# The second gate of a token mixer's merge: from the Fourier map to the merge

## The chip, the cores and the metric

The kernel runs on one core of a Trainium2 chip. The metric is the device time of one execution in microseconds (us). The engines are named as in the profile: PE is TensorE, DVE is VectorE, ACT is ScalarE, POOL is GpSimd, SP is SyncE. SP, ACT and POOL each have a queue from which DMA transfers are issued in program order.

## The reference

One layer over 2048 latent tokens of width 1024, in float32. What bears on the change is the merge of two token-mixing branches:

```python
p = h @ w_in                                   # one projection for both branches and both gates
attn = attend(q, k, v)                         # latent attention, 8 heads
four = Re(FFT2(p[..., OFF_F:OFF_GA]))          # over positions and over 128 channels of each group
ga = sigmoid(p[..., OFF_GA:OFF_GB])
gb = sigmoid(p[..., OFF_GB:N_IN])
x = x + g1 * ((ga * (attn @ w_o_attn) + gb * (four @ w_fourier)) @ w_out)
# then a second norm, a router and 16 experts of 256 tokens each
```

## The kernel before

The kernel runs in stages, each with its own pools of buffers. The order of the instructions on each engine comes from a scheduler, which follows the written order and moves an instruction up where its buffers allow it.

The input stage (0 to 640 us) projects the tokens with transposed outputs: rows are channels. It writes both gates to the scratch tensors `ga_d` and `gb_d`, 8 blocks of 128 channels by 2048 tokens each. `finish` evacuates a PSUM tile through ACT with a sigmoid, or through DVE without one, and stores it from ACT's queue. For the last five of the eight `gb` blocks the last 512 tokens are projected later, by `gates` in the next stage, and for all eight they are stored without the sigmoid.

Around 640 to 870 us the queries, keys and values are made, and the cosine and sine sums over the positions (`Spectrum`) run beside them.

The Fourier map (L918 to L957) finishes the branch. For each of 8 column blocks `j`, three pieces of 342 frequencies are made: 6 matmuls into `po` (odd part), copied by ACT to `zo`, and 7 matmuls into `pe` (even part). DVE then writes `pe - zo` and `pe + zo` into the halves of `z` (L938, L943). `po` and `pe` have three PSUM buffers each, `z` three, `zo` two. The gate block `gb` (1 MB, two buffers) is loaded by SP (L925), its last quarter gets its sigmoid on ACT (L944), POOL multiplies `z` by it (L945), and ACT's queue stores `z` to `z_d` (L946). In between stand, by program order, the folds of the map's weights for the next blocks (`fold_w`), the split of the first head's keys and values into two parts (`load_kv`, ACT and POOL) and steps of `row_max`, the row maxima of the first query block: score matmuls into `S` (L907) and a maximum on DVE (L908).

The attention (960 to 1832 us) runs 32 groups of 18 key tiles.

The merge (1832 to 2160 us) works in 8 blocks `b` of 256 tokens. For each of four pairs of channel blocks `merge` runs 24 matmuls into `p`, multiplies by `ga` (L1206), adds the gated Fourier branch `zz` (L1207) and splits the sum into `mh` (ACT) and `ml` (DVE). `project` multiplies by `w_out`; the second norm and the router of the previous block lie between. `gates` (L1150) loads `ga` from ACT's queue and `zz` from SP's; both have two buffers, and only the first two pairs are asked for ahead of time (L1158). In the first block the last five rows of `w_out` are loaded, multiplied by a gain on POOL (L1162) and split.

Of the kernel before, what the change touches and what calls it, by code (L numbers as in the profile page):

```python
# [11 lines left out]
F = mybir.dt.float32  # L12
# [5 lines left out]
AF = mybir.ActivationFunctionType  # L18
OP = mybir.AluOpType
# [5 lines left out]
T = 2048  # L25
# [85 lines left out]
def layer_kernel(ctx: ExitStack, tc: tile.TileContext, a: dict, out: bass.AP, stop: str = ""):  # L111
    nc = tc.nc

    def pool(es, name, bufs=1, **kw):
        return es.enter_context(tc.tile_pool(name=name, bufs=bufs, reuse_waits="tile", **kw))
# [14 lines left out]
    gb_d = dr.tile([8, 128, T], F, name="gb_d")  # L130
    z_d = dr.tile([8, 128, T], F, name="z_d")
# [21 lines left out]
    def mm3(ps, terms, extra=()):  # L153

        n = len(terms)
        for i, (lh, ll, rh, rl) in enumerate(terms):
            nc.tensor.matmul(ps, lh, rh, start=i == 0, stop=False)  # L157
            nc.tensor.matmul(ps, lh, rl, start=False, stop=False)  # L158
            nc.tensor.matmul(ps, ll, rh, start=False, stop=i == n - 1 and not extra)  # L159
        for i, (l, r) in enumerate(extra):  # L160
            nc.tensor.matmul(ps, l, r, start=False, stop=i == len(extra) - 1)
# [35 lines left out]
    def load_w(wp, j):  # L197
        raw = wp.tile([128, D], F, name="wraw", bufs=1)
        nc.sync.dma_start(raw, a["w_in_t"][j])
        hi = wp.tile([128, D], R, name="whi")  # L200
        lo = wp.tile([128, D], R, name="wlo")
        split(hi, lo, raw, "a")
        return [x.rearrange("p (k c) -> p k c", k=8) for x in (hi, lo)]

    def terms(w, g):
        return [(w[0][:, k], w[1][:, k], hT[g][0][:, k, :], hT[g][1][:, k, :]) for k in range(8)]

    def finish(ps, g, dst, func=None):

        n = 512 if g < 4 else 256  # L210
        o = st.tile([128, 512], F, name="oA")
        if func is None:
            nc.vector.tensor_copy(o[:, :n], ps[:, :n])
        else:
            nc.scalar.activation(o[:, :n], ps[:, :n], func)
        nc.scalar.dma_start(dst, o[:, :n])

    def tokens(g):
        return slice(g * 512, min((g + 1) * 512, NK))

    def dst_of(j, g):
        if j < 3:
            return cq_d[j, :, tokens(g)]
        return ckv_d[j - 3, :, tokens(g)]

    def gate_dst(j, g):
        return (ga_d if j < 8 else gb_d)[j % 8, :, tokens(g)]

    with ExitStack() as es:
# [7 lines left out]
        def proj(w, g, dst, func=None):  # L237
            n = 512 if g < 4 else 256
            ps = psm.tile([128, 512], F, name="mm")
            mm3(ps[:, :n], terms(w, g))  # L240
            finish(ps, g, dst, func)
# [25 lines left out]
        with ExitStack() as es2, ExitStack() as es_mod, ExitStack() as es_x:  # L267
# [3 lines left out]
            mp = pool(es_mod, "modw", 2, side="right")  # L271
# [115 lines left out]
        with ExitStack() as es2:  # L387
            mp = pool(es2, "mod", 1, side="right")
# [59 lines left out]
            w = load_w(wp, order[0])  # L448
            for n, j in enumerate(order):
                nxt = load_w(wp, order[n + 1]) if n + 1 < len(order) else None  # L450
                if 5 <= j < 9:
                    fourier_fold(j - 5, w)
                elif j < 5:
                    for g in range(4):
                        proj(w, g, dst_of(j, g))
                else:
                    for g in range(4 if j < 20 else 3):
                        proj(w, g, gate_dst(j - 9, g), AF.Sigmoid if j < 17 or g < 3 else None)
                        next(rows, None)
                        next(rows, None)  # L460
                w = nxt
# [72 lines left out]
    with ExitStack() as es:  # L534
# [10 lines left out]
        def gates():  # L545

            for j in range(20, 25):
                w = load_w(wp, j)
                ps = psm.tile([128, 512], F, name="mm")
                mm3(ps, terms(w, 3))  # L550
                finish(ps, 3, gate_dst(j - 9, 3))
                yield

        gate_steps = gates()

        def load_up(name, g, kt, n):
# [187 lines left out]
        ahead = front(0)  # L744
        rows = None
        for t in range(NK // 128):
# [37 lines left out]
            if t % 2 and t + 1 < NK // 128:  # L784
                ahead = front(t + 1)
# [11 lines left out]
    with ExitStack() as es:  # L797
# [50 lines left out]
        def shift_row(i):  # L848

            for c in range(0, NK, 576):  # L850
                nc.vector.memset(kh[i][96:97, c:c + 576].bitcast(F), -1.0)
                yield
                yield
# [65 lines left out]
        with ExitStack() as es2:  # L919
            gp = pool(es2, "gz", 2)  # L920
            psz = pool(es2, "psZ", 1, space=PSUM)
            for j in range(8):
                c = slice(j * 128, (j + 1) * 128)
                gb = gp.tile([128, T], F, name="gb")
                nc.sync.dma_start(gb, gb_d[j])  # L925
                z = gp.tile([128, T], F, name="z", bufs=3)
                zo = gp.tile([128, 1026], F, name="zo")
                for n in range(3):
                    k0 = n * 342
                    k = slice(k0, k0 + 342)  # L930
                    po = psz.tile([128, 512], F, name="po", bufs=3)
                    mm3(po[:, :342], [(WM[0][:, t, c], WM[1][:, t, c], OT[0][:, t, k], OT[1][:, t, k]) for t in range(2)])
                    nc.scalar.copy(zo[:, k], po[:, :342])
                    pe = psz.tile([128, 512], F, name="pe", bufs=3)
                    mm3(pe[:, :342], [(WP[0][:, t, c], WP[1][:, t, c], ET[0][:, t, k], ET[1][:, t, k]) for t in range(2)],
                        [(WN[:, c], NY[:, k])])
                    w = 342 if n < 2 else 341
                    nc.vector.tensor_tensor(z[:, k0:k0 + w], pe[:, :w], zo[:, k0:k0 + w], op=OP.subtract)  # L938
                    u0 = 1 if n == 0 else 0
                    w = 342 if n < 2 else 340  # L940
                    hi = T - (k0 + u0)
                    lo = T - (k0 + w)
                    nc.vector.tensor_tensor(z[:, hi:lo:-1], pe[:, u0:w], zo[:, k0 + u0:k0 + w], op=OP.add)  # L943
                nc.scalar.activation(gb[:, 1536:], gb[:, 1536:], AF.Sigmoid)  # L944
                nc.gpsimd.tensor_tensor(z, z, gb, op=OP.mult)  # L945
                nc.scalar.dma_start(z_d[j], z)  # L946
                if j < 2:
                    fold_w(j + 2)
                if j == 1:
                    for _ in load_kv(0):  # L950
                        pass
                    load_q(0)
                    load_q(1)
                    for _ in shift_row(0):
                        pass
                for _ in range(0 if j < 3 else 2 if j < 5 else 3):
                    next(first, None)  # L957
# [24 lines left out]
    with ExitStack() as es:  # L982
# [117 lines left out]
        for n in range(4 * NH):  # L1100
            nxt = row_max(n + 1) if n + 1 < 4 * NH else iter(())
# [38 lines left out]
    with ExitStack() as es:  # L1140
        wp = pool(es, "wmerge", side="right")
        mp = pool(es, "merge", 2)
# [5 lines left out]
        for k in range(3, 8):  # L1148
            wo.append((wp.tile([128, D], R, name=f"woh{k}"), wp.tile([128, D], R, name=f"wol{k}")))
        def gates(b, j):  # L1150
            ga = mp.tile([128, 2, 256], F, name="ga")
            zz = mp.tile([128, 2, 256], F, name="zz")
            tb = slice(b * 256, (b + 1) * 256)
            nc.scalar.dma_start(ga, ga_d[j:j + 2, :, tb].rearrange("j p t -> p j t"))
            nc.sync.dma_start(zz, z_d[j:j + 2, :, tb].rearrange("j p t -> p j t"))
            return ga, zz

        ahead = [gates(0, 0), gates(0, 2)]  # L1158
# [33 lines left out]
        def merge(b):  # L1192

            tb = slice(b * 256, (b + 1) * 256)
            if b:
                at = at0 if b % 2 == 0 else at1
                nc.sync.dma_start(at, o_d[:, tb].rearrange("(k p) t -> p k t", p=128))
                split(ats[0], ats[1], at, "a")
            ms = (mp.tile([128, 8, 256], R, name="mh", bufs=1), mp.tile([128, 8, 256], R, name="ml", bufs=1))
            for j in range(0, 8, 2):  # L1200
                ga, zz = ahead.pop(0) if ahead else gates(b, j)
                ps = ps1.tile([128, 2, 256], F, name="p1")
                for i in range(2):
                    c = slice((j + i) * 128, (j + i + 1) * 128)
                    mm3(ps[:, i], [(woa[0][:, k, c], woa[1][:, k, c], ats[0][:, k], ats[1][:, k]) for k in range(4)])
                nc.vector.tensor_tensor(ga, ps, ga, op=OP.mult)  # L1206
                nc.vector.tensor_tensor(ga, ga, zz, op=OP.add)  # L1207
                split(ms[0][:, j:j + 2], ms[1][:, j:j + 2], ga, "a")
            return ms
# [106 lines left out]
    with ExitStack() as es:  # L1316
# [147 lines left out]
        for n in range(16):  # L1464
            t = (0, 6, 1, 2, 7, 10, 3, 11, 8, 4, 12, 13, 9, 5, 14, 15)[n]
            for u in range(2):
                nc.tensor.matmul(pi[u], oa[:, t, u].rearrange("p a e -> p (a e)"), ob[:, t, u], start=n == 0, stop=n == 15)
        for u in range(2):
# [3 lines left out]
            with nc.allow_low_precision("whole numbers below 2048"):  # L1472
# [4 lines left out]
                                    op=OP.mult)  # L1477
# [131 lines left out]
```

## Time and profile before

| what | value |
|---|---|
| median of 3 runs | 2821.38 us (2820.79 to 2821.4) |
| the profiled execution: its time | 2819.62 us |
| the profiled execution: its span | 2817.8 us |
| PE busy | 2673.2 us (95% of the span) |
| DVE, ACT, POOL busy | 1810.0, 1398.9, 1018.2 us |
| HBM read and written | 256.59 and 87.08 MB |

The span is the time from the first to the last instruction that the profiler recorded; the execution's own time is 1.8 us longer. A busy share says little about one stage: it is an average over stages with different limits. So the stages are read one by one, and in each the wait that ends last.

### The profile page before, as it was taken

To read this page: it belongs to the slowest core of one execution; us is meant where nothing else is said; L and a number is where in the kernel's file an instruction comes from. 1 tells how busy PE (TensorE), PEld (TensorE's weight loads), DVE (VectorE), ACT (ScalarE), POOL (GpSimd) and SP (SyncE) were. 2 spreads that over 40 slices of the span, in tenths; PEclk is the share of its full clock that TensorE was granted. 3 is DMA by queue.
4 is the path that set the end of the run, shared out by engine and by line. 5 is a ranking of instruction groups with operands and counts; after the bars stand their busy time and mean duration, and the time that the engine had idled before them with its cause. 6 is when DMAs were issued, how large, how long until landed. Compare 5 with 4: busy or idle time off the path is not lost.

```text
span 2817.8 us, 39391 instructions
## 1 busy us (share of the span) xinstructions
PE 2673.2 (95%) x14160; PEld 2209.0 (78%) x14160; DVE 1810.0 (64%) x3272; ACT 1398.9 (50%) x2437; POOL 1018.2 (36%) x840
## 2 busy tenths in 40 slices
PE   6999999999998899999999999999996699999997
PEld 4878777787877677777777777788885599999996
DVE  6632133005667699999999999775556666666663
ACT  6511111114665488888888888722234344444441
POOL 2000000002545688788788787810003311111110
PEclk9999999999999999999999999999998799999999
DMA  6220244124667411011011100164444578787773
GB/s 226 105 78 29 98 159 151 68 82 135 184 180 227 169 31 39 21 38 37 23 49 38 33 23 13 55 214 140 146 136 143 166 227 241 230 234 229 232 224 63
DMA packets 201354, 346.25 MB, mean 123 GB/s; under 512 B 56751, under 2 KB 111731, under 8 KB 199110
## 3 DMA queue, kind: packets, MB, share of 16 engines
q1 hardware_dynamic: 151958, 235.52, 26.9%
q0 software_dynamic: 14832, 46.55, 7.3%
q10 hardware_dynamic: 34368, 61.66, 6.1%
q8 instruction: 111, 1.82, 0.3%
q14 instruction: 85, 0.70, 0.1%
HBM read 256.59 MB, written 87.08 MB: 122 GB/s over the span
## 4 chain that ended last, share of the span: by engine, by line
PE 79%; DMA 7%; DVE 7%; issue 3%; POOL 2%; ACT 2%; SPq 0%; POOLq 0%; ACTq 0%; DVEq 0%
PE mm L157 6%; PE mm L158 6%; PE mm L159 6%; PE S L907 5%; PE P L1083 4%; PE P L1084 4%; PE P L1082 4%; PE Ob L1023 4%; PE Oa L1022 4%; PE pa L158 4%; PE pa L159 4%; PE pa L157 4%; PE p L157 3%; PE p L159 3%; PE p L158 3%
## 5 line engine op out<-in xcount | busy, mean ns | idle before, releaser
L147 POOL TENSOR_TENSOR acc<-acc,phi 128x512 f32<-128x512 f32 x384 | 495.6, 1291 | 77.1 <-ACT phi L143 57.8
L144 DVE TENSOR_TENSOR plo<-P,phi 128x512 fp32r<-128x512 f32 x576 | 385.5, 679 | 20.9 <-ACT phi L143 18.9
L908 DVE TENSOR_REDUCE mxs<-S 128x1 f32<-128x1024 f32 (+1 forms) x384 | 365.7, 952 | 45.8 <-PE S L907 39.2
L1085 ACT ACTIVATE P<-P 128x512 f32<-128x512 f32 x576 | 328.9, 586 | 72.1 <-PE P L1084 68.4
L143 ACT CAST ewhi<-ewraw 128x1024 fp32r<-128x1024 f32 x181 | 190.1, 1050 | 312.8 <-PE pa L158 191.6
L143 ACT CAST phi<-P 128x512 fp32r<-128x512 f32 x576 | 327.7, 593 | 16.1 <-ACT P L1085 0.7
L157 PE MATMUL mm<-hh,whi 128*128 128x512 f32 (+1 forms) x792 | 312.5, 396 | 0.0
L158 PE MATMUL mm<-hl,whi 128*128 128x512 f32 (+1 forms) x792 | 311.3, 394 | 0.0
L159 PE MATMUL mm<-hh,wlo 128*128 128x512 f32 (+1 forms) x792 | 310.0, 392 | 0.0
L144 DVE TENSOR_TENSOR ewlo<-ewraw,ewhi 128x1024 fp32r<-128x1024 f32 x181 | 219.0, 1222 | 131.5 <-ACT ewhi L143 131.4
L158 PE MATMUL pa<-xTl,ewhi 128*128 128x256 f32 x1024 | 290.5, 284 | 3.8 <-DVE xTl L144 3.6
L157 PE MATMUL pa<-xTh,ewhi 128*128 128x256 f32 x1024 | 291.2, 285 | 0.0
L159 PE MATMUL pa<-xTh,ewlo 128*128 128x256 f32 x1024 | 289.4, 283 | 0.0
L1082 PE MATMUL P<-qh,kh 97*128 97x512 f32 x576 | 230.2, 400 | 1.3 <-DVE qh L914 1.3
L1083 PE MATMUL P<-ql,kh 96*128 96x512 f32 x576 | 228.7, 397 | 0.0
L1084 PE MATMUL P<-qh,kl 96*128 96x512 f32 x576 | 228.2, 396 | 0.0
L907 PE MATMUL S<-kh,qh 96*128 96x512 f32 (+1 forms) x640 | 200.0, 377 | 17.5 <-DVE mxs L908 13.9
L1023 PE MATMUL Ob<-plo,vv 128*66 128x512 f32 x576 | 215.8, 400 | 0.2 <-DVE plo L144 0.2
L1022 PE MATMUL Oa<-phi,vv 128*128 128x512 f32 x576 | 214.9, 399 | 1.0 <-ACT phi L143 1.0
L615 POOL TENSOR_TENSOR ckv<-ckv 128x256 f32<-128x256 f32 x9 | 6.9, 762 | 567.7 <-ACT ckv L613 567.7
L158 PEld LDWEIGHTS pa<-xTl,ewhi 128*128 128x128 f32 x1024 | 193.8, 189 | 9.9 <-DVE xTl L144 7.7
L157 PEld LDWEIGHTS pa<-xTh,ewhi 128*128 128x128 f32 x1024 | 193.3, 189 | 2.2 <-ACT xTh L143 0.2
(499 smaller groups left out, 5864.0 us busy)
## 6 DMA issues: line engine op xcount, KB each, us to landing
ewraw<-in_w_gate_t_dram SPq DMA_DIRECT2D x64, 512.0 KB
ewraw<-in_w_up_t_dram SPq DMA_DIRECT2D x64, 512.0 KB
ewraw<-in_w_e_down_dram SPq DMA_DIRECT2D x64, 512.0 KB
wmr<-in_w_mod_dram SPq DMA_DIRECT2D x64, 256.0 KB
wraw<-in_w_in_t_dram SPq DMA_DIRECT2D x30, 512.0 KB
wm<-in_w_mod_t_dram SPq DMA_DIRECT2D x32, 256.0 KB
ga_d<-oA ACTq DMA_DIRECT2D x32, 256.0 KB
gb_d<-oA ACTq DMA_DIRECT2D x32, 256.0 KB
```

What stands on the lines that cost most here:

```text
L143: (nc.scalar.copy if eng == "a" else nc.vector.tensor_copy)(hi, src)
L144: nc.vector.tensor_tensor(lo, src, hi.bitcast(F), op=OP.subtract)
L147: nc.gpsimd.tensor_tensor(o, x, y, op=op)
L157: nc.tensor.matmul(ps, lh, rh, start=i == 0, stop=False)
L158: nc.tensor.matmul(ps, lh, rl, start=False, stop=False)
L159: nc.tensor.matmul(ps, ll, rh, start=False, stop=i == n - 1 and not extra)
L907: nc.tensor.matmul(S[:, d:e], q[:96, j * 128:(j + 1) * 128], k[:96, c0 + d:c0 + e], start=True, stop=True)
L908: nc.vector.tensor_reduce(mxs[:, c:c + 1], S[:, :w], axis=AX.X, op=OP.max)
L1082: nc.tensor.matmul(S, k[:, c], qh, start=True, stop=False)
L1083: nc.tensor.matmul(S, k[:96, c], ql, start=False, stop=False)
L1084: nc.tensor.matmul(S, l[:, c], qh[:96], start=False, stop=True)
L1085: nc.scalar.activation(S, S, AF.Exp)
```

## The change

In the input stage every gate tile that is projected there now gets its sigmoid on the way out. Only the last 512 tokens of the last five `gb` blocks are still stored without it. The map loads just these (`gl`, five tiles of 256 KB), takes the sigmoid, and stores them back to `gb_d` from POOL's queue. The map's result goes to `z_d` ungated, also from POOL's queue; the load of 1 MB per block and the product on POOL are gone there. The merge loads `gb` beside `ga` and `zz`, with three buffers each, and POOL multiplies `zz` by it. Each pair is asked for two pairs ahead, across block borders.

```diff
@@ input stage
-                        proj(w, g, gate_dst(j - 9, g), AF.Sigmoid if j < 17 or g < 3 else None)
+                        proj(w, g, gate_dst(j - 9, g), AF.Sigmoid)
@@ Fourier map
+            gl = [gp.tile([128, 512], F, name=f"gl{j}", bufs=1) for j in range(3, 8)]
+            for j in range(3, 8):
+                nc.sync.dma_start(gl[j - 3], gb_d[j, :, 1536:])
             for j in range(8):
                 c = slice(j * 128, (j + 1) * 128)
-                gb = gp.tile([128, T], F, name="gb")
-                nc.sync.dma_start(gb, gb_d[j])
...
-                nc.scalar.activation(gb[:, 1536:], gb[:, 1536:], AF.Sigmoid)
-                nc.gpsimd.tensor_tensor(z, z, gb, op=OP.mult)
-                nc.scalar.dma_start(z_d[j], z)
+                nc.gpsimd.dma_start(z_d[j], z)
+                if j > 2:
+
+                    nc.scalar.activation(gl[j - 3], gl[j - 3], AF.Sigmoid)
+                    nc.gpsimd.dma_start(gb_d[j, :, 1536:], gl[j - 3])
@@ merge
         def gates(b, j):
-            ga = mp.tile([128, 2, 256], F, name="ga")
-            zz = mp.tile([128, 2, 256], F, name="zz")
+            ga = mp.tile([128, 2, 256], F, name="ga", bufs=3)
+            gb = mp.tile([128, 2, 256], F, name="gb", bufs=3)
+            zz = mp.tile([128, 2, 256], F, name="zz", bufs=3)
             tb = slice(b * 256, (b + 1) * 256)
+            nc.sync.dma_start(gb, gb_d[j:j + 2, :, tb].rearrange("j p t -> p j t"))
             nc.scalar.dma_start(ga, ga_d[j:j + 2, :, tb].rearrange("j p t -> p j t"))
             nc.sync.dma_start(zz, z_d[j:j + 2, :, tb].rearrange("j p t -> p j t"))
+            nc.gpsimd.tensor_tensor(zz, zz, gb, op=OP.mult)
             return ga, zz
...
-                ga, zz = ahead.pop(0) if ahead else gates(b, j)
+                ga, zz = ahead.pop(0)
+                nxt = b * 4 + j // 2 + 2
+                if nxt < T // 64:
+                    ahead.append(gates(nxt // 4, nxt % 4 * 2))
```

The scheduler moves instructions with it. On ACT, from the third column block of the map on, before (`qh` and `vv` are splits of the first queries and values):

```order
L933 COPY zo<-po 128x342 x3
L944 ACTIVATE gb<-gb 128x512 x2
L150 CAST vv_7148<-vraw 128x6x64
L933 COPY zo<-po 128x342
L150 CAST qh<-qraw 96x512
L933 COPY zo<-po 128x342
L946 DMA z_d<-z 128x2048
L933 COPY zo<-po 128x342 x2
```

and now, at the same place and up to the attention's table load:

```order
L150 CAST kh_7146<-kraw 96x384 x2
L948 ACT_TABLE_LOAD
L948 ACTIVATE gl_7200<-gl_7200 128x512
L143 CAST wph<-wt 128x2x256
L934 COPY zo<-po 128x342 x2
L143 CAST wmh<-xc 128x2x256
L150 CAST vv_7148<-vraw 128x6x64
L948 ACTIVATE gl_7201<-gl_7201 128x512
L948 ACTIVATE gl_7202<-gl_7202 128x512
L934 COPY zo<-po 128x342
L948 ACTIVATE gl_7203<-gl_7203 128x512
L948 ACTIVATE gl_7204<-gl_7204 128x512
```

The sigmoids now stand together in the middle of the map, behind two key copies; the stores of `z` have left ACT's queue, and after one more copy of queries fifteen `zo` copies follow each other.

On POOL, from the start of the map, before (`kl`, `vv`, `ql` are the low parts of keys, values and queries):

```order
L812 MEMSET vv_7148 128x18x2
L945 TENSOR_TENSOR z<-z,gb 128x2048
L147 TENSOR_TENSOR kl_7147<-kraw,kh_7146 96x384 x2
L945 TENSOR_TENSOR z<-z,gb 128x2048
L147 TENSOR_TENSOR kl_7147<-kraw,kh_7146 96x384 x4
L147 TENSOR_TENSOR vv_7148<-vraw,vv_7148 128x6x64 x2
L147 TENSOR_TENSOR ql<-qraw,qh 96x512 x2
```

and now:

```order
L147 TENSOR_TENSOR kl_7147<-kraw,kh_7146 96x384 x4
L945 DMA z_d<-z 128x2048
L147 TENSOR_TENSOR kl_7147<-kraw,kh_7146 96x384
L147 TENSOR_TENSOR vv_7148<-vraw,vv_7148 128x6x64
L147 TENSOR_TENSOR kl_7147<-kraw,kh_7146 96x384
L147 TENSOR_TENSOR vv_7148<-vraw,vv_7148 128x6x64
L147 TENSOR_TENSOR ql<-qraw,qh 96x512
L945 DMA z_d<-z 128x2048
```

The products are gone, and the stores of `z` stand between the splits; the five gate stores (L949) follow a little later, ahead of the third store of `z`.

On SP, at the start of the merge (`x` is first a buffer for rows of `w_out`), before:

```order
L1180 DMA rc<-in_norm_g_dram 128x8x1
L1155 DMA zz<-z_d 128x2x256 x2
L1161 DMA x<-in_w_out_dram 128x1024 x3
L1155 DMA zz<-z_d 128x2x256 x2
L1175 DMA h_18019<-in_norm_g_dram 128x1024
```

and now:

```order
L1186 DMA rc<-in_norm_g_dram 128x8x1
L1158 DMA gb<-gb_d 128x2x256
L1160 DMA zz<-z_d 128x2x256
L1158 DMA gb<-gb_d 128x2x256
L1160 DMA zz<-z_d 128x2x256
L1167 DMA x<-in_w_out_dram 128x1024 x3
L1158 DMA gb<-gb_d 128x2x256
```

Two gate loads have come ahead of the weights. POOL's products stand likewise: two of `zz` before the first three of `x`, one between these and the last two, and one behind them.

## Rows read from the trace of the kernel before

**Rows 1.** Stages; columns: stretch, length, busy of PE PEld DVE ACT POOL, PEclk, DMA

```profile
865.00:960.00 95.00, 74.46 (x388) 67.32 (x387) 64.12 (x106) 36.10 (x73) 54.78 (x28) 0.89 0.72 245
...
1832.00:2160.00 328.00, 312.61 (x1813) 269.33 (x1811) 199.78 (x395) 94.83 (x150) 25.27 (x25) 0.97 0.46 149
```

**Rows 2.** The same view, slices of 5 us inside the map

```profile
885.00:890.00 5.00, 3.14 (x18) 2.85 (x17) 4.94 (x7) 0.45 (x1) 3.94 (x3) 0.93 0.57 172
...
915.00:920.00 5.00, 1.82 (x12) 1.54 (x11) 0.44 (x2) 0.00 (x0) 4.28 (x1) 1.00 0.95 398
```

**Rows 3.** Waits around the map: who <- for whom, total us, times, longest

```profile
ACT gb L944 <- DMA gb<-gb_d: 23.0, 5, 6.2
...
DVE z L938 <- ACT zo L933: 18.0, 6, 5.8
...
PE S L907 <- DVE mxs L908: 11.3, 5, 5.7
...
ACT L1085 <- POOL z L945: 8.3, 1, 8.3
```

**Rows 4.** Timeline of PE: start, length, engine, line, operation, [idle before <- releaser]

```profile
873.17 0.42 PE L157 MATMUL po<-oth,wmh 128*128 128x342 f32 x1 [1.70 <-ACT wmh L143]
...
943.09 0.62 PE L907 MATMUL S<-kh,qh 96*128 96x512 f32 x2
...
943.55 0.32 PE L157 MATMUL pe<-eth,wph 128*128 128x342 f32 x1
...
946.70 0.63 PE L907 MATMUL S<-kh,qh 96*128 96x512 f32 x2
...
953.80 0.76 PE L1082 MATMUL P<-qh,kh 97*128 97x512 f32 x1 [1.06 <-DVE qh L914]
```

**Rows 5.** Timeline of ACT at the end of the map

```profile
955.75 0.33 ACTq L946 DMA_DIRECT2D z_d<-z  x1
...
956.16 1.28 ACT L1085 ACT_TABLE_LOAD   x1 [8.26 <-POOL z L945]
...
957.46 1.07 ACT L1085 ACTIVATE P<-P 128x512 f32<-128x512 f32 x2
```

**Rows 6.** Timelines of POOL and DVE, fold and gate early in the map

```profile
876.45 0.69 DVE L144 TENSOR_TENSOR wml<-xc,wmh 128x512 fp32r<-128x512 f32 x1
...
881.34 4.78 POOL L945 TENSOR_TENSOR z<-z,gb 128x2048 f32<-128x2048 f32 x1 [0.17 <-ACT wph L143]
...
881.55 5.11 DVE L144 TENSOR_TENSOR wpl<-wt,wph 128x512 fp32r<-128x512 f32 x1
```

**Rows 7.** Timeline of POOL: first sum of the attention after the map

```profile
959.77 1.26 POOL L147 TENSOR_TENSOR acc<-phi 128x512 f32<-128x512 f32 x1 [1.45 <-DMA z_d<-z]
```

**Rows 8.** Loads issued by POOL: issue ns min/median/max; then size and us to landing

```profile
L491 POOL DMA_DIRECT2D tabx<-in_c_so_dram x4: 729/736/743, 825.4 to 854.6; - x4
...
tabx<-in_c_so_dram POOLq DMA_DIRECT2D x4, 512.0 KB, 6.2
```

**Rows 9.** Page, groups: POOL additions of 128x512

```profile
L147 POOL TENSOR_TENSOR acc<-acc,phi 128x512 f32<-128x512 f32 x384 | 495.6, 1291 | 77.1 <-ACT phi L143 57.8
```

**Rows 10.** Merge, first block: slice of 8 us, then timelines of POOL and DVE

```profile
1852.00:1860.00 8.00, 5.15 (x14) 3.80 (x15) 7.96 (x6) 2.60 (x4) 5.42 (x2) 0.71 0.91 269
...
1840.20 7.96 POOL L1162 TENSOR_TENSOR x<-x,g 128x1024 f32<-128x1024 f32 x3 [6.88 <-DMA x<-in_w_out_dram]
...
1843.04 2.87 DVE L1207 TENSOR_TENSOR ga<-ga,zz 128x512 f32<-128x512 f32 x1
```

**Rows 11.** Merge, later blocks: slice, then timelines of DVE and PE

```profile
1932.00:1940.00 8.00, 6.14 (x23) 4.54 (x23) 4.45 (x13) 2.13 (x3) 0.00 (x0) 0.83 0.54 180
...
1933.56 0.69 DVE L1206 TENSOR_TENSOR ga<-p,ga 128x512 f32<-128x512 f32 x1 [2.29 <-DMA ga<-ga_d]
...
2012.91 0.68 DVE L144 TENSOR_TENSOR ml<-ga,mh 128x512 fp32r<-128x512 f32 x1
...
2015.01 0.39 PE L159 MATMUL p<-woh,ml 128*128 128x512 f32 x1
```

## The prediction

> **What bounds the kernel now.** I read the stages first. TensorE (PE) is busy 74.46 of the 95 us around the Fourier map at a mean granted clock of 0.89, and 312.61 of the 328 us of the merge [rows 1]; nowhere else does the change move anything but the order of a few rows. So there are 20.5 us of idle PE, and some lost clock, to be had in the map, and 15.4 us in the merge. Inside the map the slices show PE at 3.14 of 5 us from 885 and 1.82 of 5 us from 915 [rows 2]. The waits name the cause: ScalarE (ACT) waits 23.0 us, five times, for the gate tile `gb` to land, in order to take the sigmoid of its last quarter; VectorE (DVE) then waits 18.0 us for the copy `zo`, which stands behind that sigmoid in ACT's queue; PE waits 11.3 us for DVE's row maxima, which stand behind the `z` additions [rows 3]. It is one chain: load, sigmoid, copy, addition, PSUM buffer free, matmul. The load itself waits for one of two `gb` buffers, which the GpSimd (POOL) product gives back. A second wait comes early: a fold subtraction of DVE with both inputs in SBUF takes 0.69 us alone, but 5.11 us when it starts 0.2 us after a POOL product of 4.78 us [rows 6]. At the stage's end ACT waits 8.3 us for the last product, because the store of `z` stands in its queue; so the first exponentials start at 957.46, although the first scores were started at 953.80 [rows 3 to 5].
>
> **The map, term by term.** From the first map matmul at 873.17 to the first score matmul at 953.80 are 80.6 us [rows 4]. What PE has to do in it: 24 pieces of 13 matmuls, 312; from 943.55 to 946.70 stand 20 of them without a wait, 0.1575 us each [rows 4], so 49.1 us. The row maxima of the first query block take 8 pairs of 512 columns at 0.46 us (943.09 to 943.55 [rows 4]) and 4 singles at half of that, 4.6 us; with four transposes some 0.5 us more. Work: 54.2 us. The other 26.4 us are waits and low clock.
>
> Removed are the eight loads of 1 MB, the eight products and the eight stores in ACT's queue; with them goes every wait of the chain above, and the blocked folds. What is late next: (a) the tail after the last map matmul, now 946.70 to 953.80 [rows 4], 7.1 us, of which one pair, one single and the transposes, 1.2 us by the figures above, are work; part of the other 5.9 is the backlog on DVE, so I keep 4 us of waiting. (b) ACT copies the keys in program order ahead of the `zo` of the third column block, so it waits for a key load that starts only when POOL has split the first chunk; three `po` buffers cover most of it; I take 2 us. (c) `z` has three buffers, and a buffer is free when its store has landed. The stores now stand in POOL's queue, behind splits of keys and five small gate stores. An issue there takes 0.74 us, and a 512 KB load of that queue lands in 6.2 us on a busy memory system [rows 8]; the same 1 MB store from ACT was issued at 955.75 and had landed by 959.77, 4.0 us [rows 5, 7]. By these two rows the new store takes 4 to 12 us (twice the half-size load); I take 6, since the map leaves the memory system freer. A buffer comes round after three blocks of 39 matmuls, 18.4 us, and a few maxima, some 20 us; I take 0.5 us of wait. Sum: 54.2 + 4 + 2 + 0.5 = 60.7, a gain of 19.9 us; rounded for smaller misses to **19**. Bounds: 54.2 + 4 = 58.2 gives 22.4; with every store at 12 us and the key wait at 6 us it is some 69, a gain of 12.
>
> The exponentials can then follow the first scores without the 1.28 us table load and the store in front of them [rows 5]. That is up to 2 us, but four score buffers hide part of it, and the first low parts of the probabilities may lie where the last `z` waits for its store, which costs up to 2 us. I take 0.5 us of gain, bounds -2 to +2. In the input stage three evacuations move from DVE to ACT beside PE's matmuls: nothing, as both engines idle there; uncovered they would be 3 x 0.6 us. The attention is PE's own, with other neighbours in its queues: 0, give or take 1.
>
> **The merge.** Added are 32 loads of 256 KB, 32 POOL products of 128x512 elements at 1.29 us each (41 us; a POOL operation of that size is the nearest row [rows 9]) and third buffers. In the first block the product stands in front of everything: POOL does two of them before the weight products `x`, one between, one after, and the `x` loads stand behind two more gate loads in SyncE's queue. There POOL and DVE already take turns: three weight products run from 1840.20 to 1848.2, an addition that is normally 0.69 takes 2.87 us, and PE idles 2.85 us of the slice at 1852 [rows 10]. The price lies between 0 (the loads land while POOL waits for `x`, 6.88 us [rows 10]) and all four products plus 1 us of loads, 6.2 us; I take 3.
>
> In the seven later blocks the third buffers and the early loads remove waits like the 2.29 us for `ga` at 1933.56, which left PE idle 1.86 us [rows 11]: a gain of about 2 in all. Against it stands the port. The rows show that a DVE operation with both inputs in SBUF waits out a POOL product [rows 6, 10]. The Trainium skill says the same as a rule (SBUF — State Buffer, "Who interferes with whom"): a DVE instruction with two SBUF inputs and a GpSimd instruction that reads SBUF exclude each other for the whole instruction, whoever starts first. By that rule each of the 32 new products can hold up an addition, an `ml` subtraction or a norm.
> In one undisturbed block the last `ml` ended at 2013.6 and was first used by PE at 2015.0: slack 1.4 us [rows 11]. One collision of 1.29 us per block is covered; the earlier `ga` adds to the slack. A second one would cost 7 x 1.2 = 8 us. I take 0.5. Merge in sum: +3 - 2 + 0.5 = **+1.5**, bounds -4 to +14.
>
> **Sum.** -19 - 0.5 + 1.5 = -18 us. The profiled execution took 2819.62, so 2801.6; the median of the runs is 1.76 above it, so 2803.4, said as **2803.5**.
>
> **Rivals.**
> (1) *The stores keep the map late.* POOL works its queue in order, so `z` of the first blocks leaves only after the key splits, and five small stores go before the third. If each store takes 12 us, DVE finds no `z` buffer in blocks 3 to 5 and the map gains 12 instead of 19; the merge's terms stay. -12 + 1.5 = -10.5, about 2811. For it: 13 issues in POOL's queue where none were; against it: the 20 us from buffer to buffer.
> (2) *The port gives the gain back, and more.* Each merge product runs while DVE wants the port, four times in every block: 7 x (4 x 1.29 - 1.4) = 26 us, and 6 us in the first block, without the 2 us of gain: +32. With the map's -19.5 that is +12.5, about 2834, slower than before. It decides once the merge loses more than 25 us, which is over 3.2 collisions per block if the start costs 6. With 2.5 to 3 per block (7 x (3.2 - 1.4) = 13 to 7 x (3.9 - 1.4) = 17, and the start 5) the sum is -2 to +3, no change. For it: the addition of 2.87 us in rows 10; against it: two of the four products of a block fall, by the loads that release them, into the projection, where DVE has little to do. By the Trainium skill's rule as it stands this rival is what should happen to those products that meet a DVE operation; the time is the one worked out here.
> (3) *The loads also relieve the merge.* The products hide, the first block is no later, and the clock stays up in the map: -22 - 1 - 3, about 2796.
> (4) *The early loads do nothing* that the buffers did not give already: then the 2 us of the later blocks are missing, 2805.5; this lies inside the forecast.
>
> **How the numbers follow.** Forecast with (4), 2798 to 2808.5: 0.62. Rival (1), 2808.5 to 2815.5: 0.17. Rival (3), below 2798: 0.08. Rival (2): about no change 0.07, slower 0.06. A measurement of this kernel can tell about 0.2%, 5.6 us, from no change: faster means below 2815.7. So faster 0.62 + 0.17 + 0.08 = 0.87, same 0.07, slower 0.06. The range leaves out rival (2) and the lower half of (3): 2796 to 2815.
>
> **What would show it.** In the changed profile the map should have no ACT wait for a gate before a `zo`, PE idle of under 10 us and its first score matmul near 934; the exponentials should follow it within 2 us. If `z` additions wait for a DMA, rival (1) is at work. In the merge, many additions or `ml` subtractions of near 2 us, and PE waiting for `ml`, would show rival (2). A merge that is longer than 328 us by over 5, or shorter by over 4, would make the merge term wrong. The whole is wrong if the stretch from the first map matmul to the first score does not shrink by at least 12 us.

## The result and the profile after

The changed kernel takes 2835.57 us (median of 7 runs, 2830.39 to 2846.08), the kernel before, run beside it, 2821.38 (7 runs, 2813.62 to 2827.96): a ratio of 1.0051, interval 1.003 to 1.0072. It is slower by half a per cent, where 18 us less were forecast.

The stages are cut at the same instructions in both traces: the first map matmul, the first and the last score matmul `P`, the transposition of `aff` that ends the merge, the first `pa` matmul of the experts.

| stretch | before, us | after, us | difference | forecast |
|---|---|---|---|---|
| up to the first map matmul | 873.2 | 876.8 | +3.6 | 0 |
| map | 80.6 | 64.9 | -15.7 | -19 |
| attention | 867.7 | 898.8 | +31.1 | -0.5 |
| last score matmul to the end of the merge | 336.4 | 345.0 | +8.6 | +1.5 |
| routing | 62.6 | 62.4 | -0.2 | 0 |
| experts | 597.3 | 596.4 | -0.9 | 0 |

The sum is +26.5 us and not +14.2, because the profiled execution of after (2846.08 us) was the slowest of its seven, while that of before was 1.8 us under its median. The first line is no effect of the change: in the eight traces below it lies between 868.9 and 876.7 us in the six that have the changed input stage, and at 869.1 and 872.7 in the two that have the old one.

So the map gained somewhat less than was forecast, and a stage that the diff does not touch lost twice as much. The view of stretches for the map, the attention and the merge (length, busy time of PE, PEld, DVE, ACT, POOL with counts, granted clock, DMA share, GB/s), first before, then after:

```profile
873.20:953.80 80.60, 62.27 (x336) 57.78 (x337) 55.00 (x86) 26.84 (x54) 49.08 (x22) 0.90 0.69 235
953.80:1821.50 867.70, 862.21 (x3790) 660.15 (x3791) 794.54 (x1224) 712.66 (x1350) 697.39 (x560) 1.00 0.13 34
1821.50:2157.90 336.40, 321.99 (x1864) 276.44 (x1862) 202.98 (x401) 99.25 (x159) 29.97 (x25) 0.97 0.46 148
```

```profile
876.80:941.70 64.90, 57.02 (x336) 54.64 (x336) 51.92 (x86) 25.41 (x51) 21.97 (x27) 0.95 0.64 216
941.70:1840.50 898.80, 879.18 (x3790) 662.97 (x3791) 787.44 (x1224) 719.91 (x1350) 696.43 (x559) 0.98 0.12 32
1840.50:2185.50 345.00, 321.88 (x1864) 273.99 (x1862) 214.33 (x401) 99.02 (x159) 75.13 (x57) 0.98 0.52 169
```

In the attention PE has the same 3790 records. Its idle time rose from 5.5 to 19.6 us, and its busy time by 17.0 us at a granted clock of 0.98 instead of 1.00: half of the loss is waiting, the other half the same matmuls at a lower clock after the waits.

What waits there is told by the list of waits of the attention (who, for whom, total us, times, longest), of which these rows bear on it, before:

```profile
POOL t L1075 <- DMA rb<-r_d: 20.2, 16, 3.0
ACT ah L143 <- POOL acc L147: 8.8, 8, 3.3
PE S L907 <- DVE mxs L908: 4.0, 13, 0.8
```

and after:

```profile
ACT ah L143 <- POOL acc L147: 46.8, 24, 4.9
DVE al L144 <- ACT ah L143: 25.3, 12, 4.2
POOL t L1078 <- DVE plo L144: 23.7, 7, 4.3
POOL t L1078 <- DMA rb<-r_d: 19.6, 8, 4.1
PE S L907 <- DVE mxs L908: 18.7, 13, 3.5
```

`t` is a group's output, `rb` the reciprocal of its sums, loaded by SP in 64 copies. `acc` is the running sum of a group's probabilities, `ah` and `al` are its high and low parts. The product of `t` and `rb` on POOL (L1075, now L1078) belongs to the group before. The order of POOL's queue tells what moved. Before, for one group (`ql` is a split of the next queries):

```
L147 TENSOR_TENSOR acc<-acc,phi 128x512 x12
L147 TENSOR_TENSOR ql<-qraw,qh 96x512
L1075 TENSOR_TENSOR t_10149<-t_10149,rb 64x512
L147 TENSOR_TENSOR acc<-phi 128x512
```

and after:

```
L147 TENSOR_TENSOR acc<-acc,phi 128x512 x9
L1078 TENSOR_TENSOR t_10137<-t_10137,rb 64x512
L147 TENSOR_TENSOR acc<-acc,phi 128x512 x3
L147 TENSOR_TENSOR ql<-qraw,qh 96x512
```

The product has gone ahead of the last three additions of the group in 20 of 31 cases, and ahead of the last one once. No line of the attention was edited; the scheduler moved it. Why it did is not shown. One such place on the chip, from the timelines of SP, POOL, ACT, DVE and PE after (start, length, engine, line, operation, [idle before <- releaser]):

```profile
1074.27 0.46 SPq L1070 DMA_DIRECT2D rb<-r_d  x1
...
1077.99 1.27 POOL L1078 TENSOR_TENSOR t<-t,rb 64x512 f32<-64x512 f32 x1 [4.16 <-ACT qh L150]
1079.23 3.99 POOL L147 TENSOR_TENSOR acc<-acc,phi 128x512 f32<-128x512 f32 x3
...
1083.25 0.62 ACT L143 CAST ah<-acc 128x512 fp32r<-128x512 f32 x1 [4.83 <-POOL acc L147]
...
1083.90 0.82 DVE L144 TENSOR_TENSOR al<-acc,ah 128x512 fp32r<-128x512 f32 x1 [4.13 <-ACT ah L143]
...
1085.91 1.22 PE L907 MATMUL S<-kh,qh 96*128 96x512 f32 x2 [3.43 <-DVE mxs L908]
1086.93 0.63 PE L1086 MATMUL P<-ql,kh 96*128 96x512 f32 x1
```

POOL stands still for 4.16 us until `rb` lands, 3.7 us after its issue (the row names a copy that ended just then; that it is the load is settled by e7). Behind it stand three additions, behind them `ah` in ACT's queue with the next exponentials, behind that `al` and the row maxima on DVE, and then PE. PE's next matmuls take 0.63 us, where the same one took 0.40 before the stall. Taking all rows together, whatever releaser they name, POOL stands idle in front of `t` for 40.4 us before and 66.4 us after. In front of a group's first addition such a wait is harmless: in e1 below it still adds up to 34.0 us there, and the attention loses nothing.

In the map, the rows that answer to [rows 2, 4, 5]: waits of the stretch, then DVE, PE and ACT.

```profile
PE pe L157 <- DVE z L944: 4.3, 1, 4.3
```

```profile
895.16 3.73 DVE L144 TENSOR_TENSOR wml<-xc,wmh 128x512 fp32r<-128x512 f32 x1
...
901.20 0.66 PE L157 MATMUL pe<-eth,wph 128*128 128x342 f32 x1 [4.31 <-DVE z L944]
...
941.74 0.77 PE L1085 MATMUL P<-qh,kh 97*128 97x512 f32 x1 [1.06 <-DVE qh L914]
...
943.43 1.28 ACT L1088 ACT_TABLE_LOAD   x1 [8.15 <-PE P L1087]
944.73 0.58 ACT L1088 ACTIVATE P<-P 128x512 f32<-128x512 f32 x1
```

No wait for a gate is left in it, and of 18.3 us of idle PE (80.60 - 62.27) 7.9 remain (64.90 - 57.02). In the merge, the groups of DVE and POOL (busy us, mean ns), first before, then after:

```profile
L1207 DVE TENSOR_TENSOR ga<-ga,zz 128x512 f32<-128x512 f32 x32 | 25.7, 805 | 0.6
...
L1243 DVE TENSOR_TENSOR h<-h,wraw 128x1024 f32<-128x1024 f32 x14 | 17.1, 1220 | 0.2
```

```profile
L1216 DVE TENSOR_TENSOR ga<-ga,zz 128x512 f32<-128x512 f32 x32 | 29.4, 920 | 2.2 <-POOL zz L1161 1.2
...
L1252 DVE TENSOR_TENSOR h<-h,wraw 128x1024 f32<-128x1024 f32 x14 | 22.8, 1626 | 0.2
...
L1161 POOL TENSOR_TENSOR zz<-zz,gb 128x512 f32<-128x512 f32 x32 | 47.6, 1496 | 224.9 <-DVE h L1251 115.7 <-DMA zz<-z_d 80.5 <-DVE ga L1215 11.2
```

With the same 401 instructions DVE is busy 214.33 us instead of 202.98: two groups with both inputs in SBUF have grown by 3.7 and 5.7 us, and POOL's products take longer than their size would (1496 ns; 1291 ns is POOL's mean for an addition of that size [rows 9]).

### The profile page after: what moved, and what is told of

The parts are those of the page before. It is cut to its first block, busy times and chain, and to the rows that moved or that the text cites. A ratio compares the mean times of both kernels' runs of the same rounds, so it can differ in the third digit from the quotient of the medians.

```text
span 2844.3 us, 39571 instructions
## 1 busy us (share of the span) xinstructions
PE 2686.0 (94%) x14160; PEld 2208.0 (78%) x14160; DVE 1813.3 (64%) x3269; ACT 1405.9 (49%) x2437; POOL 1035.4 (36%) x877
## 3 DMA queue, kind: packets, MB, share of 16 engines
q1 hardware_dynamic: 160230, 236.84, 26.8%
## 4 chain that ended last, share of the span: by engine, by line
PE 50%; DVE 7%; POOL 4%; issue 3%; DMA 3%; ACT 2%; SPq 0%; POOLq 0%; DVEq 0%; ACTq 0%
PE S L907 4%; PE pa L158 4%; PE pa L159 4%; PE pa L157 4%; PE P L1085 4%; PE P L1086 4%; PE P L1087 4%; PE Oa L1025 4%; PE Ob L1026 4%; POOL acc L147 2%; PE p L159 2%; PE p L158 2%; PE p L157 2%; PE py L1555 2%; PE py L1557 2%
## 5 line engine op out<-in xcount | busy, mean ns | idle before, releaser
L158 PEld LDWEIGHTS pa<-xTl,ewhi 128*128 128x128 f32 x1024 | 194.2, 190 | 11.4 <-DVE xTl L144 9.0
```

## The experiments

Two theories stood at the start. **O**: the place of `t`'s product in POOL's queue costs the attention its 31 us. **W**: the other rows that the scheduler moved there cost them. For the merge: **P**, the products hold DVE up, against **L**, the added loads do. In the table the stretches are cut as above; a ratio is to the kernel before, run on the same chip beside it (a median of 2816.76 to 2818.15 us beside e1 to e8). Each stretch comes from one trace. e4 leaves out the merge's second gate, e7 the division by the sums; the others compute the whole result.

| kernel | us | ratio, 95% interval | map | attention | merge |
|---|---|---|---|---|---|
| before | 2821.38 | | 80.6 | 867.7 | 336.4 |
| after | 2835.57 | 1.0051 (1.003, 1.0072) | 64.9 | 898.8 | 345.0 |
| e1: `t` late | 2808.03 | 0.9966 (0.9951, 0.998) | 65.5 | 864.6 | 346.2 |
| e2: `t` later | 2806.91 | 0.9964 (0.9951, 0.9977) | 66.3 | 867.8 | 345.8 |
| e3: store alone | 2852.22 | 1.0135 (1.0114, 1.0155) | 85.4 | 897.1 | 337.5 |
| e7: `t` early, no wait | 2807.16 | 0.995 (0.9932, 0.9967) | 66.2 | 866.4 | 345.7 |
| e4: no product | 2792.33 | 0.9926 (0.9905, 0.9947) | 66.3 | 865.0 | 332.3 |
| e5: product on DVE | 2791.88 | 0.9905 (0.9888, 0.9921) | 66.3 | 865.0 | 332.1 |
| e8: ahead alone | 2814.59 | 0.9988 (0.9974, 1.0001) | 81.2 | 865.4 | 330.9 |
| e6: gate in the map | 2810.1 | 0.9967 (0.9956, 0.9978) | 79.8 | 865.2 | 329.8 |

**e1.** The product is put where it stood before, by an order that the scheduler must keep:

```diff
-                yield
-                yield
-                yield
-                yield
-                nc.gpsimd.tensor_tensor(t[0], t[0], rb, op=OP.mult)
+                tc.keep_in_program_order(nc.gpsimd.tensor_tensor(t[0], t[0], rb, op=OP.mult))
```

> The changed kernel with one thing held: the attention's rescaling product of POOL (t by rb, L1078) is kept three additions later in POOL's queue, in front of the first addition of a group, where it stands in the kernel before. All else of the change stays, and hardly a row moves on ACT and DVE. Theory O (the order): the product, put in front of the last three additions of most groups, waits there for the load of rb; the additions, the copy ah, the exponentials and the row maxima wait behind it. Then the attention returns from 899 us to 867 to 870 us, PE's waits for the row maxima there from 18.7 to under 6 us, and the time is the median of the changed kernel less 18 to 30 us: 2806 to 2818, faster than before or about the same. Rival W (wider): the other instructions that the scheduler moved on ACT and DVE in the attention cost the 31 us; then the attention stays at 890 us or more, and the time above 2828.

Measured: 2808.03 us, and 864.6 us for the attention. PE's wait for the row maxima in that stretch, 18.7 us in after, is now:

```profile
PE S L907 <- DVE mxs L908: 1.4, 3, 0.9
```

The attention is even a little shorter than the 867 to 870 us expected. W falls. It was a serious rival: by the traces, some 157 of DVE's 1224 operations in the attention, 193 of ACT's 1350 and 22 of POOL's stand in another place of their queue after than before. From after to e1 only 3, 6 and 22 move, and the whole loss is gone. By the ratios (1.0051 - 0.9966) the place of this one instruction costs about 24 us in a typical execution.

**e2.** As e1, with all seven `yield` kept, so that the product follows four key tiles later.

> The same with the product four key tiles later still, behind the fourth addition of the group, where rb should have landed long before. Theory O: POOL's wait for rb (some 20 us in 16 waits in the kernel before, harmless there) goes away, and the attention takes the same 867 to 870 us as with the product in front of the group, within 2 us, since that wait held up nothing that PE needs; time within 3 us of the run with the product in front of the group. Rival: the wait in front of the group also cost PE something; then the attention is 3 us or more shorter and so is the time.

POOL no longer stands idle in front of `t` at all; the time is that of e1 within 1.1 us, and the attention is 3.2 us longer, not shorter, at 867.8 about the same as before. So the wait in front of the group cost nothing that can be seen.

**e3.** One part alone, in the kernel before:

```diff
-                nc.scalar.dma_start(z_d[j], z)
+                nc.gpsimd.dma_start(z_d[j], z)
```

> The kernel before with one part of the change alone: the map's result, still gated, is stored from POOL's queue in place of ACT's. With it the scheduler moves the rescaling product three additions forward in the same groups as in the changed kernel. Theory O: the attention becomes 885 to 900 us, the map gets 0 to 8 us shorter (the store no longer holds ACT up, the load of the gate still does), the merge stays at 336 us: time 2828 to 2845, slower than before. Rival N: the loss in the attention came from the rest of the change (ungated map, gate loads, lookahead); then the attention stays at 868 us and the time at 2812 to 2822.

The attention takes 897.1 us, as O says: another edit, the same order of all operations there as in the changed kernel, the same loss. As the map is longer here and not shorter, a map that is shorter on the chip is not what moves `t`. The map, however, got 4.8 us longer, and so the time is above the range. There the rows of DVE and POOL show why:

```profile
892.66 2.90 POOL L147 TENSOR_TENSOR kl<-kraw,kh 96x384 fp32r<-96x384 f32 x3
895.53 1.81 POOL L147 TENSOR_TENSOR vv<-vraw,vv 128x384 fp32r<-128x384 f32 x2
897.31 2.47 POOL L147 TENSOR_TENSOR ql<-qraw,qh 96x512 fp32r<-96x512 f32 x2
...
893.37 6.96 DVE L144 TENSOR_TENSOR wml<-xc,wmh 128x512 fp32r<-128x512 f32 x1
...
902.64 0.66 PE L157 MATMUL pe<-eth,wph 128*128 128x342 f32 x1 [11.73 <-DVE z L943]
```

A subtraction that takes 0.69 us alone [rows 6] ends only when POOL's seven splits are through, and PE then has idled 11.7 us.

**e7.** The changed kernel with the product early in every group (the nine `yield` between the store of `r_d` and the product are gone; in the trace it is ahead of three additions in 30 of 31 groups), and nothing to wait for:

```diff
-                nc.gpsimd.tensor_tensor(t[0], t[0], rb, op=OP.mult)
+                tc.keep_in_program_order(nc.gpsimd.tensor_tensor(t[0], t[0], t[0], op=OP.mult))
```

> The changed kernel with the attention's rescaling product early in all groups (three additions ahead of a group's end, where the changed kernel has it in 21 of 31), but multiplying t by itself, so that it has nothing to wait for from the load of rb (the division by the sums is left out; the load of rb is still made). Theory W (wait): the loss comes from the wait for rb alone; the attention takes 863 to 870 us and the time is that of the run with the product held late, 2803 to 2813. Rival S (slot): the product's own 1.3 us ahead of the last additions is too much for POOL, or the rest of the order is; then the attention stays at 880 us or more and the time above 2822.

Attention 866.4 us, time 2807.16, both in the range of theory W, which here is the wait: it is the wait for `rb`, not the slot. (With one input the product is a little shorter, 1.03 us.)

**e4.** e1 without the line of the merge's product; the gate is still loaded.

> The run with the rescaling product held in front of the group, and the 32 gate products of the merge left out (the output then lacks the second gate); the gate is still loaded. Theory P (port): the products cost the merge what they hold up on DVE, about 1.2 us in each later block and some of the 4.7 us of the first; without them the merge is 334 to 338 us in place of 345, and the time 7 to 11 us under that of the run with the products. Rival L (loads): the merge is longer by the added gate loads ahead of the weights and by the order alone; then it stays at 342 to 346 us and the time within 3 us of that run.

The merge falls by 13.9 us to 332.3, more than either theory had: P in direction, and under-priced. L has little left: with all the added loads the stage is 4 us shorter than before, and only 1.4 us longer than that of e8, which asks ahead as early and loads no gate.

**e5.** e1 with the product on DVE:

```diff
-            nc.gpsimd.tensor_tensor(zz, zz, gb, op=OP.mult)
...
+                ga, gb, zz = ahead.pop(0)
+                nc.vector.tensor_tensor(zz, zz, gb, op=OP.mult)
```

> As the run with the rescaling product held (2808.0, merge from the last score matmul to the router's end 346 us), with the merge's 32 gate products on DVE, each just ahead of its pair's matmuls, in place of POOL. Without any product this stage took 332 us and the kernel 2792.3, so the products on POOL cost 14 us. Theory P (port): on POOL they cost that by holding up DVE operations with both inputs in SBUF; on DVE they cost their own 0.7 us each, 22 us in all, most of it beside PE's matmuls: merge 333 to 340 us, time 2794 to 2802. Rival Z (late data): whoever makes the product, the sum waits for it and for its loads, and DVE's queue is the bound; then the merge is 344 us or more and the time 2806 or more.

The merge takes 332.1 us, as without any product and a little under the range. The group of DVE:

```profile
L1203 DVE TENSOR_TENSOR zz<-zz,gb 128x512 f32<-128x512 f32 x32 | 23.9, 746 | 10.8 <-DMA zz<-z_d 10.8
```

23.9 us of work on the busier engine are hidden, where 47.6 us on the idle one cost 14. What the products cost on POOL is, in large part, what they hold up on DVE: with the same 401 operations DVE is busy 216.79 us in the merge of e1 and 200.86 in that of e4. Up to the first `mh` matmul of the second block e1 takes 74.3 us and e4 67.9, from there to the end of the merge 271.9 and 264.4. In the later blocks the hold-up can be followed to PE. `x1Tl` is an input of the router's matmuls; PE's wait for it, in e1 and then in e5:

```profile
PE p L1268 <- DVE x1Tl L144: 5.2, 5, 1.2
```

```profile
PE p L1268 <- DVE x1Tl L144: 0.5, 1, 0.5
```

One of the five places in e1, from the timelines of POOL, DVE and PE:

```profile
2000.44 3.67 POOL L1157 TENSOR_TENSOR zz<-zz,gb 128x512 f32<-128x512 f32 x2 [5.36 <-DVE ga L1211]
...
2001.19 1.78 DVE L1212 TENSOR_TENSOR ga<-ga,zz 128x512 f32<-128x512 f32 x1
2002.89 1.27 DVE L144 TENSOR_TENSOR x1Tl<-p,x1Th 128x512 fp32r<-128x512 f32 x2
...
2003.62 1.24 PE L1268 MATMUL p<-x1Tl,wr 128*16 128x256 f32 x8 [1.20 <-DVE x1Tl L144]
```

An addition of 0.69 us takes 1.78 beside two products, `x1Tl` follows it in DVE's queue, and PE idles 1.20 us. In the first block the products also stand between POOL's weight products, and no run separates that order from the hold-up of DVE. This version is the fastest that computes the whole result: 0.9905 of the time before.

**e8.** The kernel before, with only the merge's three buffers and loads two pairs ahead.

> The kernel before with one part of the change alone: ga and zz of the merge with three buffers and asked for two pairs ahead; the gate stays in the map. The prediction's term was a gain of 2 us in the later blocks. Theory A: the stage from the last score matmul to the router's end goes from 336 to 331 to 334 us, as in the runs without a product on POOL, and the time falls by 2 to 5 us. Rival: the two waits that it removes are given back elsewhere; then the stage stays within 1 us of 336 and the time within 1 us of before.

The stage is 5.5 us shorter, the kernel 3.0 us (interval 0.9974 to 1.0001, so just not told from no change). For the stage other traces agree: 329.8 us in e6, which has the same merge, and 337.5 in e3, which has that of before. The term of 2 us was too small.

**e6.** e1 with the gate back in the map, but out of ACT's way: the last quarters in tiles of their own, products and store in POOL's queue, none in the merge. `w` is 2048 in the first three blocks and 1536 in the others.

```diff
+                gb = gp.tile([128, T], F, name="gb")
+                nc.sync.dma_start(gb[:, :w], gb_d[j, :, :w])
...
+                if j > 2:
+                    nc.scalar.activation(gl[j - 3], gl[j - 3], AF.Sigmoid)
+                    nc.gpsimd.tensor_tensor(z[:, w:], z[:, w:], gl[j - 3], op=OP.mult)
+                nc.gpsimd.tensor_tensor(z[:, :w], z[:, :w], gb[:, :w], op=OP.mult)
                 nc.gpsimd.dma_start(z_d[j], z)
```

> A version meant to keep both gains: the map is gated on POOL as in the kernel before, but nothing of the gate stands in ACT's way any more (the last quarters are small tiles of their own with their sigmoid early, products and store both in POOL's queue); the merge loads only ga and zz, with three buffers and two pairs ahead, and has no product; the attention's rescaling product is held in front of the group. If the map's loss in the kernel before came from ACT waiting for the gate's load, the map takes 65 to 72 us, the merge 331 to 335, the time 2790 to 2800. Rival: the 1 MB loads of the gate, or POOL's eight products of 4.8 us beside DVE's folds, cost the map by themselves; then it takes 75 us or more and the time is 2802 or more.

A miss: the map takes 79.8 us, although ACT waits for a gate only once, 3.4 us, where it waited five times and 23.0 us before [rows 3]. Three of the map's waits:

```profile
PE pe L157 <- DVE z L952: 10.3, 2, 5.2
...
ACT vv L150 <- DMA vraw<-v_d: 8.6, 1, 8.6
...
ACT gl L955 <- DMA gl<-gb_d: 3.4, 1, 3.4
```

Timelines of POOL and DVE:

```profile
897.74 1.98 POOL L147 TENSOR_TENSOR kl<-kraw,kh 96x384 fp32r<-96x384 f32 x2
899.68 4.54 POOL L957 TENSOR_TENSOR z<-z,gb 128x2048 f32<-128x2048 f32 x1
904.18 0.92 POOL L147 TENSOR_TENSOR vv<-vraw,vv 128x384 fp32r<-128x384 f32 x1
905.06 0.58 POOL L958 DMA_DIRECT2D z_d<-z  x1
...
897.98 8.14 DVE L836 TENSOR_TENSOR xc<-xc 128x512 f32<-128x512 f32 x1
```

So ACT's wait for the gate, which the prediction took for the main cause in the map, is not all of it: with most of that wait gone the map keeps nearly its old length. Over half of PE's 18.6 us of idle time, 10.3 us, stand behind folds that DVE ends late beside POOL's work. That the products alone do it is not shown: the loads of the gate are back as well, and ACT waits 8.6 us for a load of values, with `zo` copies behind it for which PE then waits 2.8 us. What the change gains in the map comes from taking away loads, products and ACT's wait together.

## Why the prediction was wrong

- **Map** (60.7 us, bounds to 69; gain 19, 12 to 22.4): within the bounds, 64.9 to 66.3 in six traces, a gain of 14 to 16. PE is busy 57.0 us and not 54.2, at a granted clock of 0.95. Of its 7.9 us of idle time 3.6 are the tail, for which 4 were taken; the key wait (2) and the wait for a `z` buffer (0.5) do not show at PE. The rest is a stall of 4.3 us behind the fold subtraction of 3.73 us, which the sum does not have: the prediction had said that the blocked folds go with the products, but POOL's splits of values and queries stand beside this one. The tells held: no wait of ACT for a gate, idle PE under 10 us; the first score matmul came at 941.7 instead of 934, 3.6 us of it from the later start.
- **Stores** (rival 1): rejected. They land in 5.6 us (6 were taken), and no `z` addition waits for a DMA.
- **Start of the exponentials** (gain 0.5, bounds -2 to +2): the size was right, the reason not. They start 3.0 us behind the first score matmul instead of 3.7; the table load of 1.28 us is still there (943.43), only the store in front of it is gone, and so the tell of 2 us did not hold.
- **Attention** ("0, give or take 1"): this step failed, by 31 us in the trace and some 24 us typically (e1). The reason given was that it is PE's own. What it left out is that the scheduler had reordered POOL's queue there, and that a queue in order, in which an instruction waits for a load, holds three other engines. The prediction weighed the order rows of the map and of the merge; of all other stages it said that "the order of a few rows" moves, and gave that no price. In the attention one product that moved up by three additions was the price.
- **Merge** (+1.5, bounds -4 to +14): 8.6 us, and 9.8 in e1; within the bounds, but over the 5 us by which the prediction itself would call the term wrong, and two errors offset each other in it. The loads ahead and the buffers give 5.5 us (e8), not 2. The products cost 13.9 us (e1 less e4), and the gate loads 1.4 (e4 less e8), where both together were put at 3.5; 6.4 of the 13.9 fall up to the second block and 7.5 behind it, where 0.5 was taken. The slack of 1.4 us for one collision per block was read at `ml`, but the products fall on the norm as well, where the operation with `wraw` went from 1.22 to 1.63 us, 14 times, which is half of DVE's extra 11.4 us, and on additions with the router's `x1Tl` behind them (e5).
- **Rival 2** (the port): the mechanism was right, and e4 and e5 show it. Its size, 32 us, was more than twice too large (13.9, e1 less e4), and it alone would not have made the kernel slower: with `t` in place 9.6 us of gain are left with the products on POOL (e1), and 26.8 with them on DVE (e5).
- **Slower at all**: "slower" had been given to rival 2 alone. The kernel is slower through an instruction that no term or rival named. Rival 3 (the products hide) and rival 4 (the early loads do nothing) fall with the numbers of the merge.

These two gains are the ratios of e1 and e5, 0.34% and 0.95% of 2821.4 us; the forecast was 18.

## What to carry to other kernels

Where a scheduler sets the order, an edit in one stage can move instructions in another: read the whole difference of order, and look first for an instruction that waits for a load and has gone up in a busy in-order queue; hold it in place. The engine with the most idle time need not be the cheapest home for an elementwise product: here products with both inputs in SBUF, put on GpSimd, cost VectorE's time as well, and on VectorE itself they were free.

## What the runs showed of the hardware

- **DVE can be held through several POOL operations in a row.** In e6 one operation took 8.14 us beside four POOL operations, in e3 6.96 us beside seven; each ended 0.5 to 1.1 us after the last of them. It is not always so: in the kernel before, the subtraction of 5.11 us [rows 6] ended 0.6 us after the one product, although POOL's next operation had begun at 886.07, with no gap. Nor does a pause of POOL always let DVE in: the subtraction of 3.73 us after, from 895.16, spans an issue of 0.59 us at 895.55 and ends behind the two splits that follow. What decides is not shown. The Trainium skill (SBUF — State Buffer, "Who interferes with whom") says that the shared pair is held for the whole instruction and that the order of issue decides; the traces agree that one holds up the other, but the measured waits in e3 and e6 are longer than any one POOL instruction there, and the measurement decides.
- **A short stall of PE costs about as much again.** After the idle 3.4 us before 1085.91 the slices of 5 us granted 0.53 of full speed, near the lower of the clock's two levels (1.2 and 2.4 GHz), and 0.79, where the slices before them had 1.00; in the whole attention 14.1 us of added idle time came with 17.0 us of slower matmuls. In e3 it was 16.8 us with 12.6. The slices, with the columns of the stretches above:

```profile
1080.00:1085.00 5.00, 2.48 (x11) 1.70 (x9) 1.10 (x2) 1.72 (x4) 4.84 (x5) 1.00 0.12 26
1085.00:1090.00 5.00, 4.09 (x10) 3.12 (x11) 3.88 (x5) 3.11 (x6) 4.37 (x4) 0.53 0.16 39
1090.00:1095.00 5.00, 5.00 (x20) 3.80 (x19) 3.50 (x6) 4.12 (x8) 3.49 (x3) 0.79 0.21 59
```

Left open: why the scheduler moves `t`, what of the first block's loss in the merge is POOL's order and what DVE's hold-up, and what decides when DVE gets its turn.
